# A decoder block's attention and forget gate rebuilt on one Trainium2 core: unsplit float32 q and k, scores on 64 rows, half-height transposes, values in one group, larger lumps

## The chip, the core and the metric

The kernel runs on one core of one Trainium2 chip. The metric is the device time of one execution in microseconds (us), the median of three runs. A profile of one execution comes with it: for each engine, when each instruction started, how long it took and what it waited for. The engines are PE (TensorE: matmuls, and PEld, its weight loads), DVE (VectorE), ACT (ScalarE), POOL (GpSimd) and SP, which issues the DMAs. Each engine works through its own queue in order.

## What is computed

One decoder layer on 256 tokens of width 1024 in float32, with two attention branches of 8 heads of 64 each:

```python
h = rms_norm(x, attn_norm_g)
qa, ka, va, qb, kb, vb, f_logit, g_logit = split(h @ w_in)
qa = rope(rms_norm(heads(qa), gq)); ka = rope(rms_norm(heads(ka), gk))   # branch 0
o_a = softmax(qa ka^T / 8, causal) va      # one block of 256 keys: plain causal attention
qb = rms_norm(heads(qb), gq2); kb = rms_norm(heads(kb), gk2)             # branch 1
c = cumsum(log_sigmoid(f_logit + b_forget))
o_b = softmax(qb kb^T / 8 + c[t] - c[s], causal) vb
x = x + (gate0 * (o_a @ w_moba) + gate1 * (o_b @ w_fox)) @ w_out
h2 = rms_norm(x, ffn_norm_g); u, g = split(h2 @ w_up)
x = x + (silu(conv3(g)) * u) @ w_down
```

## The kernel before

**Precision.** Weights and activations are split into a rounded float32r part and the rest (`whi` and `wlo`, `xh` and `xl`, `oh` and `ol`); a product is three float32r matmuls: hi by hi, hi by lo, lo by hi. ACT writes the hi part (L109 for weights), DVE the lo part (L110). Six buffers of each are in turn: a new one is split when PE has finished with the one six halves back. V, the probabilities and the transposes are plain float32. A plain float32 matmul of the code stands as two records in the trace, a transpose as one.

**Order.** PE's queue stands exactly as the code is written. The other engines' queues are laid out by a scheduler from data dependences. Weights come in chunks of 1 MB through three `raw` buffers.

**Stages on PE.** `project(m, pt, h)` does half of a 512-column projection (two weight halves, 24 matmul pairs, L212); m = 0, 1, 2 are q, k, v of branch 0, and 3, 4, 5 of branch 1. `norm1` (L190) sums the squares of x; DVE and ACT make `rs`, the row scale, of it (L177 to L182). `rs_row` (L408) spreads `rs` over a row. `forget_a` to `forget_d` and `forget_bias` make the decay bias of branch 1: `forget_a` multiplies x with the 8 forget columns (L283, L284: 16 matmuls with 16 columns of hi and lo weights), `forget_b` turns that (L293) and takes log-sigmoid, `forget_c` makes the cumulative sum (L322 to L324), `forget_d` sends it through DRAM to all partitions. `finish_qk` normalises q or k on DVE and ACT into `qn` (and for branch 0 applies rope, L237 to L240). `turn_qk` transposes it (8 transposes, L257) and writes the pieces qA, qB, kA for the split scores. `scores(br, pair)` (L362, L363) makes two heads' scores, each product in two float32r matmuls over 128 rows (hi and lo of k stacked on the rows), and then the softmax on DVE and ACT (L368 to L376); of 256 by 256 the upper right block is left out, so a head has 128 x 128 and 128 x 256. `turn(br, pair)` (L385) transposes the probabilities, six blocks of 128 x 128 a pair. `values(br, pair)` (L396) multiplies them with V, two heads side by side on 64 columns each. Then `gate(c)`, eight times, 48 float32r matmuls of 256 columns (L420 to L422).

These pieces are written between the projections and gates one pair at a time (L440 to L504), so that DVE and ACT have a projection's or a gate's time for each.

## Time and profile before

| | us |
|---|---|
| median of three runs | 386.28 |
| runs | 385.81 to 386.96 |
| span of the profiled execution (first to last instruction) | 377.5 |
| PE busy in the span | 369.2 |
| DVE, ACT, POOL busy in the span | 286.4, 227.9, 15.7 |
| branch attention and gates (45.97 to 148.62), length | 102.65 |

The profiled execution has no time of its own beside its span; the span is 8.8 us shorter than the median of the runs. A line of the timeline reads: start, length, engine, line of the code, operation, written tile <- read tiles, shape, count; several equal instructions in a row are one line, from the first start to the last end. The time in brackets is how long the engine sat idle ahead of it, and who ended that. Records of matmuls overlap, since PE takes up the next before the last has drained; so costs on PE are read from start to start.

### The profile page before, as it was taken

To read this page: it belongs to the slowest core of one execution; us is meant where nothing else is said; L and a number is where in the kernel's file an instruction comes from. 1 tells how busy PE (TensorE), PEld (TensorE's weight loads), DVE (VectorE), ACT (ScalarE), POOL (GpSimd) and SP (SyncE) were. 2 spreads that over 40 slices of the span, in tenths; PEclk is the share of its full clock that TensorE was granted. 3 is DMA by queue.
4 is the path that set the end of the run, shared out by engine and by line. 5 is a ranking of instruction groups with operands and counts; after the bars stand their busy time and mean duration, and the time that the engine had idled before them with its cause. 6 is when DMAs were issued, how large, how long until landed. Compare 5 with 4: busy or idle time off the path is not lost.

```text
span 377.5 us, 7103 instructions
## 1 busy us (share of the span) xinstructions
PE 369.2 (98%) x2893; PEld 346.9 (92%) x2893; DVE 286.4 (76%) x504; ACT 227.9 (60%) x382; POOL 15.7 (4%) x19
## 2 busy tenths in 40 slices
PE   7999999999999999999999999999999999999995
PEld 2778887879999999999999999999999999999995
DVE  3879989899987755787796968676776867778653
ACT  4938497678956795454578756454554545455520
POOL 2410000000000000000060000000000000000000
PEclk9999999999999999999999999999999999999999
DMA  6994740755363533544645545554465456545003
GB/s 200 359 368 160 258 163 7 264 184 190 138 222 126 212 114 111 208 159 192 225 153 182 214 167 184 221 214 168 178 222 198 159 202 224 194 157 207 3 0 111
DMA packets 12000, 68.11 MB, mean 180 GB/s; under 512 B 1592, under 2 KB 2240, under 8 KB 4416
## 3 DMA queue, kind: packets, MB, share of 16 engines
q1 hardware_dynamic: 11664, 66.60, 49.3%
q10 hardware_dynamic: 304, 1.06, 0.8%
q8 instruction: 22, 0.36, 0.4%
q14 instruction: 10, 0.08, 0.1%
HBM read 66.60 MB, written 1.06 MB: 179 GB/s over the span
## 4 chain that ended last, share of the span: by engine, by line
PE 86%; DVE 4%; DMA 3%; ACT 3%; SPq 1%; issue 1%; POOLq 0%; POOL 0%; ACTq 0%; DVEq 0%
PE bank L420 14%; PE bank L421 14%; PE bank L422 14%; PE bank L212 12%; PE bank L605 5%; PE bank L606 5%; PE bank L604 5%; DMA raw<-in_qkv 3%; PE bank L517 2%; PE bank L519 2%; PE bank L518 2%; DVE wlo L110 2%; PE bank L396 2%; PE bank L385 2%; PE bank L544 1%; PE bank L543 1%
## 5 line engine op out<-in xcount | busy, mean ns | idle before, releaser
L110 DVE TENSOR_TENSOR wlo<-raw,whi 128x1024 fp32r<-128x1024 f32 (+1 forms) x126 | 152.2, 1213 | 50.4 <-ACT whi L109 50.2
L109 ACT ACTIVATE whi<-raw 128x1024 fp32r<-128x1024 f32 (+1 forms) x126 | 129.1, 1029 | 84.1 <-PE bank L421 45.3
L421 PE MATMUL bank<-ol,whi 128*128 128x256 f32 x352 | 97.3, 276 | 0.1
L420 PE MATMUL bank<-oh,whi 128*128 128x256 f32 x352 | 97.4, 277 | 0.0
L422 PE MATMUL bank<-oh,wlo 128*128 128x256 f32 x352 | 97.2, 276 | 0.0
L421 PEld LDWEIGHTS bank<-ol,whi 128*128 128x128 f32 x352 | 66.1, 188 | 0.3 <-DVE ol L552 0.3
L420 PEld LDWEIGHTS bank<-oh,whi 128*128 128x128 f32 x352 | 66.1, 188 | 0.0
L422 PEld LDWEIGHTS bank<-oh,wlo 128*128 128x128 f32 x352 | 66.1, 188 | 0.0
L420 PE MATMUL bank<-xh,whi 128*128 128x256 f32 x128 | 36.2, 283 | 0.0
L422 PE MATMUL bank<-xh,wlo 128*128 128x256 f32 x128 | 35.9, 280 | 0.0
L421 PE MATMUL bank<-xl,whi 128*128 128x256 f32 x128 | 35.9, 280 | 0.0
L212 PE MATMUL bank<-whi,xh 128*128 128x512 f32 x96 | 30.6, 400 | 1.2 <-ACT whi L109 1.0
L212 PE MATMUL bank<-wlo,xh 128*128 128x512 f32 x96 | 30.3, 397 | 1.0 <-DVE wlo L110 1.0
L212 PE MATMUL bank<-whi,xl 128*128 128x512 f32 x96 | 29.8, 391 | 0.0
L422 PEld LDWEIGHTS bank<-xh,wlo 128*128 128x128 f32 x128 | 24.4, 190 | 0.0
L420 PEld LDWEIGHTS bank<-xh,whi 128*128 128x128 f32 x128 | 24.2, 189 | 0.2 <-issue 0.2
L421 PEld LDWEIGHTS bank<-xl,whi 128*128 128x128 f32 x128 | 24.0, 188 | 0.0
L212 PEld LDWEIGHTS bank<-wlo,xh 128*128 128x128 f32 x96 | 17.6, 188 | 6.6 <-DVE wlo L110 2.9
L212 PEld LDWEIGHTS bank<-whi,xh 128*128 128x128 f32 x96 | 17.2, 188 | 5.6 <-ACT whi L109 2.5
L212 PEld LDWEIGHTS bank<-whi,xl 128*128 128x128 f32 x96 | 18.0, 188 | 4.0
L573 DVE TENSOR_TENSOR sq<-bank,rs 128x512 f32<-128x512 f32 x22 | 15.1, 690 | 6.5 <-PE bank L422 6.5
L371 ACT ACTIVATE s<-s,nm 128x128 f32<-128x128 f32 (+1 forms) x32 | 14.2, 448 | 9.1 <-DVE nm L368 8.3
(171 smaller groups left out, 756.2 us busy)
## 6 DMA issues: line engine op xcount, KB each, us to landing
raw<-in_wu SPq DMA_DIRECT2D x22, 1024.0 KB, 4.8
raw<-in_wd SPq DMA_DIRECT2D x11, 1024.0 KB, 4.9
raw<-in_qkv SPq DMA_DIRECT2D x9, 1024.0 KB, 4.9
raw<-in_wg SPq DMA_DIRECT2D x8, 1024.0 KB, 5.3
raw<-in_wb SPq DMA_DIRECT2D x4, 1024.0 KB, 4.8
raw<-in_wo SPq DMA_DIRECT2D x4, 1024.0 KB, 4.7
raw<-in_qkv SPq DMA_DIRECT2D x8, 256.0 KB, 6.2
raw<-in_qkv SPq DMA_DIRECT2D x2, 512.0 KB, 6.6
```

The source lines that it names most:

```text
L109: nc.scalar.activation(hi[:, s], raw[:, s], AF.Copy)
L110: nc.vector.tensor_tensor(lo[:, s], raw[:, s], hi[:, s].bitcast(F32), op=ALU.subtract)
L212: nc.tensor.matmul(pt[t], lhs[:, k, t * P:(t + 1) * P], rhs, start=(k == 0 and i == 0), stop=(k == KT - 1 and i == 2))
L371: last_exp[:] = [nc.scalar.activation(s[:, j, c], s[:, j, c], AF.Exp, scale=-1.0, bias=nm[:, j, i:i + 1], accum_out=l[:, j, i:i + 1])]
L385: nc.tensor.transpose(tp[:, b * P:(b + 1) * P], s[:, j, b * P:(b + 1) * P], ident)
L420: nc.tensor.matmul(o, wh[:, w], mh[:, k], start=(k == 0 and i == 0), stop=False)
L421: nc.tensor.matmul(o, wh[:, w], ml[:, k], start=False, stop=False)
L422: nc.tensor.matmul(o, wl[:, w], mh[:, k], start=False, stop=(k == KT - 1 and i == 1))
L573: nc.vector.tensor_tensor(ev, up_.rearrange("p (b t) -> p b t", b=2), rs2[:, None, :].to_broadcast([P, 2, S]), op=ALU.mult)
L604: nc.tensor.matmul(o, wh[:, w], ah, start=(p == 0 and h == 0 and c == 0), stop=False)
L605: nc.tensor.matmul(o, wh[:, w], al, start=False, stop=False)
L606: nc.tensor.matmul(o, wl[:, w], ah, start=False, stop=(last and h == 1 and d == ds[-1]))
```

## The change

- q and k are no longer split: `turn_qk` writes plain float32 tiles qT and kT, one copy on ACT and one on DVE for a whole q or k (before: 24 and 16 pieces over the four calls; now 4 and 4).
- `scores` takes two pairs at a time. A head's product is one plain float32 matmul over its own 64 rows (two records in the trace); the two heads of a pair lie on the upper and the lower 64 rows, and write different banks.
- Transposes (`turn_qk`, `turn`) take 64 rows at a time: twice as many, each with 64 columns streamed instead of 128; upper and lower halves follow each other and write different banks.
- `values(br)` does all four pairs of a branch, two pairs to a bank; one copy and one subtraction then cover two pairs.
- `forget_a` uses unsplit x and weights: eight plain float32 matmuls of 32 columns, four column strips at once, placed with `rs_row` directly behind `norm1`. `forget_b` adds the four strips up with a selection matrix (`sel`, eight more columns of the constants) in two plain float32 matmuls.
- The order of the pieces is written anew; `s` and `pT` have four buffers instead of three and two. The FFN takes qT, kT and a third tile aT where it took qA, qB, kA.

```diff
-    for tag in ("qA", "qB", "kA"):
-        T([P, 2, 4, S], tag, 1, F32R)
+    for tag in ("qT", "kT", "aT"):
+        T([P, 4, S], tag, 1, F32R)
...
     def turn_qk(qn, br, isk):
         g = col(C_QG + 2 * br + isk)
-        for t in range(NT):
-            tp = bank()
+        tp = banks()
+        for t in range(NT):
             for b in range(4):
-                nc.tensor.transpose(tp[:, b * P:(b + 1) * P], qn[:, t, 2 * b:2 * b + 2].rearrange("p h d -> p (h d)"), ident)
...
-                nc.scalar.activation(hi, src, AF.Copy, scale=g[own])
...
-                nc.vector.scalar_tensor_tensor(lo, src, g[own], hi.bitcast(F32), op0=ALU.mult, op1=ALU.subtract)
+                for h, r in enumerate(halves):
+                    src = qn[r, t, 2 * b:2 * b + 2].rearrange("p h d -> p (h d)")
+                    nc.tensor.transpose(tp[h][:, (4 * t + b) * HD:(4 * t + b + 1) * HD], src, ident[r, r])
+        dst = (kT if isk else qT).rearrange("p b (t h c) -> p h t b c", t=NT, h=2)
+        for h in range(2):
+            src = tp[h].rearrange("p (t b c) -> p t b c", t=NT, b=4)
+            if h == 0:
+                nc.scalar.activation(dst[:, h], src, AF.Copy, scale=g)
+            else:
+                nc.vector.tensor_scalar_mul(dst[:, h], src, g)
...
+        wfg = T([P, KT, 32], "wfg")
+        nc.gpsimd.memset(wfg, 0.0)
+        nc.vector.tensor_tensor(wfg[:, :, 0:NH], wfr, g1[:, :, None].to_broadcast([P, KT, NH]), op=ALU.mult)
         fp = bank()
         for k in range(KT):
-            nc.tensor.matmul(fp[:16, :S], wf2[:, k], xh[:, k], start=(k == 0), stop=False)
-            nc.tensor.matmul(fp[:16, :S], wf2[:, k], xl[:, k], start=False, stop=(k == KT - 1))
+            r = slice(32 * (k % 4), 32 * (k % 4 + 1))
+            nc.tensor.matmul(fp[r, :S], wfg[:, k], xT[:, k], start=(k < 4), stop=(k >= 4))
...
-            nc.tensor.transpose(ft[:, t * 16:(t + 1) * 16], fs[:, t * P:(t + 1) * P], ident[:16, :16])
+            nc.tensor.matmul(ft[:, t * NH:(t + 1) * NH], fs[:, t * P:(t + 1) * P], sel, start=True, stop=True)
...
-                nc.tensor.matmul(dst, qA[:, j, pair, ts], kA[:, j, pair, us], start=True, stop=False)
-                nc.tensor.matmul(dst, qB[:, j, pair, ts], kA[:, j, pair, us], start=False, stop=True)
+    def scores(br, pairs):
+        sps = [banks() for _ in pairs]
+        for t in range(NT):
+            ts, us = slice(t * P, (t + 1) * P), slice(0, (t + 1) * P)
+            for pair, sp in zip(pairs, sps):
+                for j, r in enumerate(halves):
+                    nc.tensor.matmul(sp[j][:, t * P:t * P + (t + 1) * P], qT[r, pair, ts], kT[r, pair, us], start=True, stop=True)
+        for pair, sp in zip(pairs, sps):
+            softmax(br, pair, sp)
...
-                nc.tensor.transpose(tp[:, b * P:(b + 1) * P], s[:, j, b * P:(b + 1) * P], ident)
+                for h, r in enumerate(halves):
+                    nc.tensor.transpose(tp[h][:, (3 * j + b) * HD:(3 * j + b + 1) * HD], s[r, j, b * P:(b + 1) * P], ident[r, r])
...
+    def values(br):
+        for pp in range(2):
+            op = bank()
+            for i, c in enumerate((slice(0, 256), slice(256, 384))):
+                for q in range(2):
+                    pair = 2 * pp + q
+                    for j, r in enumerate(halves):
+                        vc = br * W4 + (2 * pair + j) * HD
+                        nc.tensor.matmul(op[r, q * S + i * P:(q + 1) * S], V[:, i, vc:vc + HD], probs[br, pair][:, j, c],
+                                         start=(i == 0 and q == 0), stop=(i == 1 and q == 1))
```

The new order of the calls, from `norm1` to the last gate:

```python
norm1(); rs_row(); forget_a(); qn = finish_qk(pq, 0, 0); project(1, pk, 1)
kn = finish_qk(pk, 0, 1); project(2, pv, 0); forget_b(); turn_qk(qn, 0, 0)
project(2, pv, 1); turn_qk(kn, 0, 1); finish_v(pv, 0); project(3, pq, 0)
forget_c(); scores(0, (0, 1)); project(3, pq, 1); qn = finish_qk(pq, 1, 0)
forget_d(); scores(0, (2, 3)); project(4, pk, 0); turn(0, 0); turn(0, 1)
project(4, pk, 1); kn = finish_qk(pk, 1, 1); turn(0, 2); turn(0, 3); turn_qk(qn, 1, 0)
project(5, pv, 0); forget_bias(); values(0); project(5, pv, 1); turn_qk(kn, 1, 1)
finish_v(pv, 1); gate(0); scores(1, (0, 1)); gate(1); scores(1, (2, 3)); gate(2); gate(3)
turn(1, 0); turn(1, 1); gate(4); turn(1, 2); turn(1, 3); gate(5); values(1); gate(6); gate(7)
```

Three places show what moved. First PE's queue at `norm1`, before the change (the row with L190; L212 is `project(1, pk, ...)`):

```order
L212 MATMUL bank_204<-whi_171,xl_84 128x512
L212 MATMUL bank_205<-whi_171,xl_84 128x512
L190 MATMUL bank_296<-ones1_153,bias_159 128x1 x2
L212 MATMUL bank_204<-whi_177,xh_83 128x512
L212 MATMUL bank_205<-whi_177,xh_83 128x512
L212 MATMUL bank_204<-wlo_178,xh_83 128x512
```

and now (L191 is `norm1`, L409 `rs_row`, L279 `forget_a`, L213 the projection):

```order
L213 MATMUL bank_201<-whi_171,xl_84 128x512
L213 MATMUL bank_202<-whi_171,xl_84 128x512
L191 MATMUL bank_293<-ones1_153,bias_159 128x1 x2
L409 MATMUL bank_311<-cst_185,rs_189 128x128 x2
L279 MATMUL bank_318<-xT_82,wfg_315 32x256 x8
L213 MATMUL bank_201<-whi_177,xh_83 128x512
```

`rs_row` and `forget_a` have moved ahead of the half projection that stood behind `norm1`.

Second, PE's queue at the first `turn_qk`, before: it stands (L257) at the end of `project(2, pv, 1)`, and `project(3, pq, 0)` follows.

```order
L212 MATMUL bank_207<-whi_340,xl_84 128x512
L257 MATMUL bank_519<-cst_185,qn_314 128x128 x4
L257 MATMUL bank_530<-cst_185,qn_314 128x128 x4
L212 MATMUL bank_543<-whi_358,xh_83 128x512
L212 MATMUL bank_544<-whi_358,xh_83 128x512
```

Now it stands at the end of `project(2, pv, 0)`, behind `forget_b` (L288); the first two of its 16 rows, one for each half:

```order
L213 MATMUL bank_203<-whi_259,xl_84 128x512
L213 MATMUL bank_204<-whi_259,xl_84 128x512
L288 MATMUL bank_449<-cst_185,pT_327 128x8 x2
L257 MATMUL bank_471<-cst_185,qn_329 128x64
L257 MATMUL bank_472<-cst_185,qn_329 128x64
```

It has moved a half projection forward, and with it k's `turn_qk`, which now ends `project(2, pv, 1)`.

Third, DVE's queue ahead of the first `qn`, before, from its multiplication with the norm (L230) to rope's last row (L240); L110 are weight splits, L177 and L180 belong to k:

```order
L230 TENSOR_TENSOR qn_314<-bank_202,qf_322 128x512
L230 TENSOR_TENSOR qn_314<-bank_203,qf_322 128x512
L177 TENSOR_SCALAR qfv_409<-ss_401 128x16
L110 TENSOR_TENSOR wlo_427<-raw_356,whi_426 128x1024
L237 TENSOR_TENSOR p1_334<-qn_314,rc0_306 128x256
L238 TENSOR_TENSOR p2_335<-qn_314,rsn0_307 128x256
L180 SCALAR_TENSOR_TENSOR qfv_409<-qfv_409 128x16
L110 TENSOR_TENSOR wlo_445<-raw_442,whi_444 128x1024
L239 TENSOR_TENSOR qn_314<-p1_334,p2_335 128x16x8
L240 TENSOR_TENSOR qn_314<-p1_334,p2_335 128x16x8
```

and now (L231 to L241; L226 belongs to k):

```order
L231 TENSOR_TENSOR qn_329<-bank_199,qf_337 128x512
L231 TENSOR_TENSOR qn_329<-bank_200,qf_337 128x512
L110 TENSOR_TENSOR wlo_374<-raw_371,whi_373 128x1024
L238 TENSOR_TENSOR p1_349<-qn_329,rc0_303 128x256
L239 TENSOR_TENSOR p2_350<-qn_329,rsn0_304 128x256
L226 TENSOR_REDUCE ss_390<-sq_394 128x8
L240 TENSOR_TENSOR qn_329<-p1_349,p2_350 128x16x8
L241 TENSOR_TENSOR qn_329<-p1_349,p2_350 128x16x8
```

One weight split fewer stands between, and one fewer ahead of these rows: five in place of seven from `rs` on.

More of the change, by code (lines that the diff above doesn't have):

```diff
@@ L162, in decoder_block @@
     load(7)
-    cst = T([P, 832], "cst")
+    cst = T([P, 840], "cst")
     nc.sync.dma_start(cst, a["consts"])
@@ L169, in decoder_block, with rsqrt_mean @@
     cos2 = cst[:, 768:832].rearrange("p (t c) -> p t c", t=NT)
+    sel = cst[:, 832:840]
     wfr = T([P, KT, NH], "wfr")
     nc.sync.dma_start(wfr, a["wf"])
-    def rsqrt_mean(dst, ss, n, shape, tag):
-        w = T([P, 3] + shape, tag, 2)
+    def rsqrt_mean(dst, ss, n, shape, tag, bufs=2):
+        w = T([P, 3] + shape, tag, bufs)
         v, y, t = w[:, 0], w[:, 1], w[:, 2]
@@ L351, in decoder_block, with softmax @@
     last_exp = []
-    def scores(br, pair):
-        s = T([P, 2, 384], "s", 3)
+    def scores(br, pairs):
[7 more added lines that the diff above has]
+            softmax(br, pair, sp)
+    def softmax(br, pair, sps):
+        s = T([P, 2, 384], "s", 4)
         nm = T([P, 2, 2], "nm", 4)
         l = T([P, 2, 2], "l", 4)
-        sps = banks()
-        for t in range(NT):
-            for j in range(2):
-                dst = sps[j][:, t * P:t * P + (t + 1) * P]
-                ts, us = slice(t * P, (t + 1) * P), slice(0, (t + 1) * P)
-                nc.tensor.matmul(dst, qA[:, j, pair, ts], kA[:, j, pair, us], start=True, stop=False)
-                nc.tensor.matmul(dst, qB[:, j, pair, ts], kA[:, j, pair, us], start=False, stop=True)
         for j in range(2):
@@ L444, in decoder_block @@
     norm1()
+    rs_row()
+    forget_a()
     qn = finish_qk(pq, 0, 0)
     project(1, pk, 1)
-    rs_row()
-    forget_a()
     kn = finish_qk(pk, 0, 1)
@@ L451, in decoder_block @@
     forget_b()
+    turn_qk(qn, 0, 0)
     project(2, pv, 1)
-    turn_qk(qn, 0, 0)
+    turn_qk(kn, 0, 1)
     finish_v(pv, 0)
@@ L456, in decoder_block @@
     project(3, pq, 0)
-    turn_qk(kn, 0, 1)
+    forget_c()
+    scores(0, (0, 1))
     project(3, pq, 1)
-    forget_c()
-    scores(0, 0)
     qn = finish_qk(pq, 1, 0)
+    forget_d()
+    scores(0, (2, 3))
     project(4, pk, 0)
-    forget_d()
-    scores(0, 1)
+    turn(0, 0)
+    turn(0, 1)
     project(4, pk, 1)
-    turn(0, 0)
-    scores(0, 2)
     kn = finish_qk(pk, 1, 1)
+    turn(0, 2)
+    turn(0, 3)
+    turn_qk(qn, 1, 0)
     project(5, pv, 0)
-    values(0, 0)
-    turn(0, 1)
+    forget_bias()
+    values(0)
     project(5, pv, 1)
-    scores(0, 3)
-    turn_qk(qn, 1, 0)
+    turn_qk(kn, 1, 1)
     finish_v(pv, 1)
-    values(0, 1)
-    turn(0, 2)
-    forget_bias()
     gate(0)
-    turn(0, 3)
-    turn_qk(kn, 1, 1)
-    values(0, 2)
+    scores(1, (0, 1))
     gate(1)
-    values(0, 3)
-    scores(1, 0)
+    scores(1, (2, 3))
     gate(2)
-    scores(1, 1)
     gate(3)
     turn(1, 0)
-    scores(1, 2)
+    turn(1, 1)
     gate(4)
-    values(1, 0)
-    turn(1, 1)
-    scores(1, 3)
+    turn(1, 2)
+    turn(1, 3)
     gate(5)
-    values(1, 1)
-    turn(1, 2)
+    values(1)
     gate(6)
-    values(1, 2)
-    turn(1, 3)
     gate(7)
@@ L503, in decoder_block @@
         gate_sigmoid(c)
-    values(1, 3)
     mh = T([P, KT, S], "xh", 1, F32R)
```

64 lines of the change are left out of this document (21 added, 43 removed).

## The prediction

> **What bounds the kernel now.** I read the page's busy times and its chain that ended last first, then the stretch from the first branch's attention to its end, then the timeline of TensorE (PE) in that stretch.
>
> ```profile
> span 377.5 us, 7103 instructions
> PE 369.2 (98%) x2893; PEld 346.9 (92%) x2893; DVE 286.4 (76%) x504; ACT 227.9 (60%) x382; POOL 15.7 (4%) x19
> PE 86%; DVE 4%; DMA 3%; ACT 3%; SPq 1%; issue 1%; POOLq 0%; POOL 0%; ACTq 0%; DVEq 0%
> 45.97:148.62 102.65, 102.29 (x740) 92.11 (x738) 85.42 (x203) 80.01 (x169) 0.00 (x0) 1.00 0.46 164
> ```
>
> The last row gives, for the stretch from 45.97 to 148.62 with nearly all attention in it, the busy time of PE, PEld (weight loads), DVE, ACT and POOL, then PE's granted clock. PE is busy 98% of the span and 102.29 of 102.65 us there; the clock is 1.00. So I count PE's time from one start to the next, and work of DVE and ACT only where PE waits for it. The many ACT and DVE instructions that the change drops count for nothing by themselves. Behind 148.62 (branch projections, output, FFN) PE issues the same instructions in the same order; I carry that stretch over whole.
>
> **The change, part by part.** First what the new PE order waits for.
>
> ```profile
> 25.47 0.51 PE L190 MATMUL bank<-ones,bias 128*128 128x1 f32 x4
> 25.83 0.70 PE L212 MATMUL bank<-whi,xh 128*128 128x512 f32 x2
> 27.07 0.16 DVE L182 SCALAR_TENSOR_TENSOR rs<-rsv 128x2 f32<-128x2 f32 x1
> 31.41 0.61 PE L408 MATMUL bank<-cst,rs 128*128 128x128 f32 x4
> 31.78 0.36 PE L283 MATMUL bank<-xh,wf 128*16 128x256 f32 x1
> 33.73 0.63 PE L212 MATMUL bank<-whi,xh 128*128 128x512 f32 x2
> 39.34 0.29 PE L293 MATMUL bank<-cst,pT 16*128 16x16 f32 x2
> 39.56 0.74 PE L212 MATMUL bank<-whi,xh 128*128 128x512 f32 x2
> ```
>
> *rs.* norm1's matmuls are followed at 25.83 by a projection; rs is written at 27.07 + 0.16 = 27.23. The change puts rs_row, which reads rs, directly behind norm1, and the projection behind that. PE waits from 25.83 to about 27.28: **+1.45**. Behind the waiting matmul stand forget_a, the projection and all the rest of PE's queue; DVE and ACT are free for this chain in both, and their own queues go on.
>
> *forget_a.* Today 31.78 to 33.73 = 1.95. The rate of a plain f32 matmul is L408's: four records (two per matmul written) spaced (0.61 - 0.27)/3 = 0.11 for 128 columns. New: eight matmuls of 256 columns = 4 x 0.11 = 0.44 each, four of them side by side on column strips, so two rounds, 0.88, and 0.1 to change over: **-0.95**. If only two strips ran at once it would be -0.1.
>
> *forget_b.* Today 0.22 (39.34 to 39.56). Two plain f32 matmuls with 128-column loads are four records; below, L323's two records take 0.22, so 0.44 and the gap ahead: **+0.15**. PE thus reaches turn_qk(qn) at 39.56 + 1.45 - 0.95 + 0.15 = 40.2; today it comes there a half projection later.
>
> ```profile
> 31.27:48.16 16.89, 16.89 (x90) 13.76 (x89) 16.78 (x41) 11.74 (x18) 0.00 (x0) 1.00 0.67 243
> 28.99 2.36 DVE L110 TENSOR_TENSOR wlo<-raw,whi 128x1024 fp32r<-128x1024 f32 x2 [0.26 <-ACT whi L109]
> 41.14 1.22 DVE L110 TENSOR_TENSOR wlo<-raw,whi 128x1024 fp32r<-128x1024 f32 x1
> 42.47 0.29 DVE L240 TENSOR_TENSOR qn<-p,p 128x128 f32<-128x128 f32 x1
> 45.17 1.04 PE L257 MATMUL bank<-cst,qn 128*128 128x128 f32 x8
> 45.97 0.71 PE L212 MATMUL bank<-whi,xh 128*128 128x512 f32 x2
> 47.87 0.29 DVE L240 TENSOR_TENSOR qn<-p,p 128x128 f32<-128x128 f32 x1
> ```
>
> *q's wait.* qn is ready at 42.47 + 0.29 = 42.76 today, and DVE has no gap from 31 us on (16.78 busy of 16.89 in the first row, behind PE and PEld). Between rs and this L240 stand seven splits L110 (the first two and the last are shown), in the new order five; one takes 2.36 - 1.22 = 1.14 of DVE's time, so qn comes 2.3 earlier, at about 40.5: wait **+0.3**.
>
> *k's wait.* PE then does turn_qk(qn) (0.66 by the price below) and a half projection (5.5, 33.73 to 39.34 less the gap), so it is at turn_qk(kn) at 40.5 + 0.66 + 5.5 = 46.7. Today kn is ready at 47.87 + 0.29 = 48.16, and PE asks for it only behind another half projection. DVE's list ahead of kn is nearly as long in the new order (qT's evacuation is added, two small forget steps go). PE waits about 1.5 and starts there at 48.2. Queued behind it on PE is everything else. Today's PE had qn turned and started the next projection at 45.97; so up to here **+2.2**, in which all terms above are contained. Bounds: no wait for q and k, +0.4; kn two us later, +4.2.
>
> *A wait that goes.* Scores(0, 0) waits for kA today: **-0.4**. kT's two evacuations now stand a projection ahead of their use.
>
> ```profile
> 59.31 0.30 PE L362 MATMUL bank<-kA,qA 128*128 128x128 f32 x1 [0.36 <-DVE kA L269]
> 58.09 0.37 PE L323 MATMUL bank<-lf,cst 128*128 128x8 f32 x2
> 58.31 0.37 PE L324 MATMUL bank<-lf,cst 128*128 128x8 f32 x2
> 103.67 0.28 PE L422 MATMUL bank<-xh,wlo 128*128 128x256 f32 x1
> 103.89 0.87 PE L396 MATMUL bank<-pT,V 128*64 128x256 f32 x8
> 104.69 0.33 PE L362 MATMUL bank<-kA,qA 128*128 128x128 f32 x1
> 105.71 0.28 PE L420 MATMUL bank<-xh,whi 128*128 128x256 f32 x1
> 111.36 0.22 PE L362 MATMUL bank<-kA,qA 128*128 128x128 f32 x1
> 112.29 0.28 PE L420 MATMUL bank<-xh,whi 128*128 128x256 f32 x1
> ```
>
> *values.* One call writes eight records: four of 256 and four of 128 columns, 12 x 0.11 = 1.32 if each followed the last; PE is through in 0.80 (103.89 to 104.69). So the two 64-column strips do run side by side (0.66), and 0.1 goes at either end. With the gap ahead (103.79 to 103.89) a call costs 0.9, eight 7.2. New, per branch: 24 x 0.11 = 2.64 per strip and 0.2 for the ends, twice: 5.7. **-1.5**, the change-overs.
>
> *scores.* A head pair costs 1.02 (104.69 to 105.71) and 0.93 (111.36 to 112.29); eight some 7.6. New: each head has 64 rows to itself; 128 + 256 columns in two records each, 6 x 0.11 = 0.66, both heads at once; a lump of two pairs 1.32 and 0.15 to change over, four lumps 5.9: **-1.7**. The trace shows strips side by side in columns only, not in rows. Bounds: no overlap, 11.2 (+3.6); overlap of streams but not of loads (0.11 each by L323, two by two 0.22, four times a head pair), 7.6 (no gain). I take the overlap because it is nearest to L396.
>
> *Transposes.* Eight whole ones take 0.80 (45.17 to 45.97), 0.11 each; 72 remain behind turn_qk(kn)'s start, 7.8. Each becomes two of 64 rows and 64 columns.
>
> ```profile
> 39.34 0.20 PEld L293 LDWEIGHTS bank<-cst,pT 16*128 16x128 f32 x2 [0.36 <-DVE qfv L177]
> L385 PEld LDWEIGHTS bank<-cst,s 128*128 128x128 f32 x48 | 5.3, 140 | 1.0 <-DVE gates L427 0.3 <-issue 0.2 <-DVE nm L368 0.2
> L293 PE MATMUL bank<-cst,pT x2: 207/218/230, 39.3 to 39.4; 16*128 16x16 f32 x2
> ```
>
> Call T the time of two halves. The stream is half as long: 0.055 if both run at once, the lower bound. The load stays 128 columns: L293's two loads (16 rows) start 0.20 - 0.14 = 0.06 apart, and a whole one in L385 is as long (140 ns), so a load costs 0.06 however few rows: T = 0.12 if the halves load in turn. L293's two matmuls start 0.29 - 0.207 = 0.08 apart (the later is the shorter): T = 0.16 if each half costs that. I take T = 0.07, nearest to the overlap seen in L396, with a little for twice the instructions. 72 x 0.07 = 5.0, and seven lumps at 0.15: 6.1, **-1.7**.
>
> The Trainium skill, "TensorE: Matmul & The Clock Gate", section "LDWEIGHTS (loading the stationary operand)", speaks against this part: a load's time goes by its columns, 128 / 1.2 = 107 ns, and 32 rows take as long as 128. On the rows the trace agrees (L293 beside L385); on the figure it agrees for plain f32 (L323, 0.11) and not for transposes (0.06). By its figure T would be 0.107 at best and this part +1.0 where I have -1.7, so the sum -0.4.
>
> Everything that leaves ACT and DVE (20 of 24 q and k copies on ACT, 12 of 16 on DVE, half of the oh and ol splits) lies beside PE's work, and costs PE nothing there. pT and s get four buffers, so the four pairs of a branch wait for no older one. forget_d's two DMAs stay on ACT's queue, half a projection earlier, and its buffer, one of the three raw ones, is held until forget_bias as before; eight more columns of the constants are nothing in a load of 832.
>
> Sum: 2.2 - 0.4 - 1.5 - 1.7 - 1.7 = **-3.1**. The profiled span of 377.5 becomes 374.4. The median of the three runs is 386.28, 8.8 above the span, start and end that the trace does not hold; with the same 8.8 I get **383.2**.
>
> **The rivals.**
>
> *Slower: the halves do not overlap.* Place: scores and every transpose. Point: with the other terms as they are, T over 0.113 makes the kernel slower. If only loads follow one another, T = 0.12 (9.7, +1.9) and scores gain nothing: 2.2 - 0.4 - 1.5 + 0 + 1.9 = +2.2, **388.5**. If the streams do too, scores are +3.6: +5.8, **392.1**. Against it: L396's overlap. For it: no two records of the trace share the array by rows. The Trainium skill, same page, "Part 3: Packing small matmuls — row/col tiling", says that loads overlap running matmuls when the row group differs; no run here shows that yet, and it takes chance from this rival.
>
> *Each half costs an issue of 0.08.* T = 0.16, 12.6, +4.8 on the transposes: +3.4, **389.7**. For it: L293's spacing. Against: L396's eight records and eight loads pass in 0.80, 0.05 for each of the sixteen, and their streams set that.
>
> *The load sets the spacing.* T = 0.11, as a whole transpose: 9.0, +1.2, sum -0.2, **386.1**, no change.
>
> *The waits grow.* DVE is busy 85.42 of 102.65 us from 45.97, and two pairs' softmax must now be done before a lump of turns. If kn comes two us later, or turn(0, 2) waits as long for DVE, -3.1 becomes -0.5 to -1: **385.6**.
>
> **How the numbers follow.** Forecast 0.54; the halves do not overlap 0.14; issue 0.08; load spacing 0.11; waits 0.13. Within the forecast the time goes from 380.3 (T = 0.055, another -1.1, and no wait for q and k, -1.8) to 385. 0.3% is 1.16 us, about what a measurement of this kernel can tell from no change. Faster by more: nearly all of the forecast and a part of waits, 0.59. Within: load spacing, most of waits, 0.19. Slower: 0.22. The range reaches from 380.2 to 388.5; it leaves out the streams in turn, issue, and a tail below.
>
> **What would show it.** L409 (rs_row) with 1.4 us of PE idle ahead; L257 waiting for DVE's qn, some 0.3 and 1.5; 16 records of L257 in about 0.6 and 24 of L381 in 0.85 (0.07 a pair) against 0.88 and 1.3 (0.11); eight score matmuls (16 records) in 1.3 against 2.6; L395's 32 records in 2.7. The prediction fails if halves start only after one another, if PE stands before turn(0, 2), or if something behind 148.62 moves by more than the sum.

## The result, and the profile after

| us | before | after |
|---|---|---|
| executions compared first | 386.28, 385.81, 386.96, 387.15 | 385.49, 384.85, 376.54, 377.91 |
| median | 386.62 | 381.38 |
| span of the profiled execution | 377.5 | 383.7 |

The four executions of before against the two lower ones of after gave a ratio of 0.976 (0.973 to 0.979): 9.2 us faster, where 3.1 were forecast. The new times fall into two groups 8 us apart, and a number of this case can be understood only with that: executions of either kernel come in a lower and an upper group, and what lies between the groups is not the change.

The first sign stands in the page of the kernel after. Its profiled execution is 6 us longer than the one of before, though the kernel is faster.

```profile
span 383.7 us, 7223 instructions
PE 373.3 (97%) x2975; PEld 348.9 (91%) x2975; DVE 277.8 (72%) x486; ACT 214.4 (56%) x357; POOL 14.2 (4%) x18
PE 80%; DVE 9%; DMA 5%; ACT 3%; issue 1%; SPq 1%; POOLq 0%; POOL 0%; ACTq 0%; DVEq 0%
```

PE is still what bounds it. The table of stretches shows where the 6 us are. Columns: stretch, its length, busy time and (number of records) of PE, PEld, DVE, ACT, POOL, then PE's granted clock, DMA share, GB/s. First three stretches of before, then the same of after: norm1 to the first k turn, from there to the branch outputs, from there to the FFN's second block.

```profile
25.47:45.97 20.50, 20.50 (x108) 16.81 (x106) 18.70 (x46) 13.16 (x21) 0.00 (x0) 1.00 0.62 225
45.97:148.55 102.58, 102.22 (x739) 92.05 (x737) 85.42 (x203) 79.94 (x169) 0.00 (x0) 1.00 0.46 164
148.55:198.71 50.16, 49.59 (x434) 49.19 (x433) 39.23 (x55) 27.95 (x42) 7.61 (x7) 1.00 0.51 181
```

```profile
26.03:48.60 22.57, 20.17 (x117) 15.92 (x115) 20.84 (x55) 14.90 (x26) 0.00 (x0) 1.00 0.53 200
48.60:146.64 98.04, 97.67 (x809) 85.92 (x809) 73.90 (x177) 64.35 (x141) 0.00 (x0) 1.00 0.47 168
146.64:198.16 51.52, 51.06 (x434) 50.86 (x432) 39.75 (x55) 28.69 (x41) 7.71 (x7) 1.00 0.52 186
```

The first two stretches are where the change is: +2.07 and -4.54, so -2.5. The third has the same 434 matmuls in both kernels and takes 1.4 longer. One stretch of the FFN, of before and of after:

```profile
300.00:350.00 50.00, 50.00 (x444) 50.00 (x442) 36.52 (x50) 26.78 (x38) 0.00 (x0) 1.00 0.54 190
```

```profile
300.00:350.00 50.00, 50.00 (x427) 50.00 (x426) 34.90 (x49) 25.75 (x36) 0.00 (x0) 1.00 0.52 183
```

PE is busy for all 50 us in both, at clock 1.00, with the same instructions, and 444 matmuls fall into them in the one and 427 in the other: 0.113 us from start to start against 0.118. Over the 1535 matmuls from 199 us to the end that is 6.8 us (199.36 to 373.23 against 198.82 to 379.49). Nothing is waited for. I call these the two paces; a block of 48 matmuls takes 5.44 at the one and 5.65 at the other.

The places that the prediction named, in the timeline of PE after:

```profile
26.03 0.51 PE L191 MATMUL bank<-ones,bias 128*128 128x1 f32 x4
27.85 0.71 PE L409 MATMUL bank<-cst,rs 128*128 128x128 f32 x4 [1.31 <-DVE rs L183]
28.49 1.07 PE L279 MATMUL bank<-xT,wfg 128*32 128x256 f32 x16
29.49 0.73 PE L213 MATMUL bank<-whi,xh 128*128 128x512 f32 x2
...
40.59 0.51 PE L288 MATMUL bank<-cst,pT 128*128 128x8 f32 x4
41.16 0.71 PE L257 MATMUL bank<-cst,qn 64*128 64x64 f32 x16
41.80 0.73 PE L213 MATMUL bank<-whi,xh 128*128 128x512 f32 x2
...
48.60 0.71 PE L257 MATMUL bank<-cst,qn 64*128 64x64 f32 x16 [1.02 <-DVE qn L241]
...
62.97 1.58 PE L351 MATMUL bank<-kT,qT 64*128 64x128 f32 x16
64.48 0.72 PE L213 MATMUL bank<-whi,xh 128*128 128x512 f32 x2
...
70.18 0.96 PE L381 MATMUL bank<-cst,s 64*128 64x64 f32 x24
71.07 0.73 PE L213 MATMUL bank<-whi,xh 128*128 128x512 f32 x2
...
84.47 2.82 PE L395 MATMUL bank<-pT,V 128*64 128x256 f32 x32
87.22 0.74 PE L213 MATMUL bank<-whi,xh 128*128 128x512 f32 x2
```

They stand nearly as named, but q's wait of 0.3 is missing (0.07): 1.3 us of idle ahead of rs_row, 1.0 ahead of the k turn, 16 half transposes in 0.64, 24 in 0.89, a lump of scores in 1.51, a branch's values in 2.75.

### The profile page after: what moved, and what is told of

Read it like the earlier page. It is cut to its first block, busy times and chain, and to the rows that moved or that the text cites. A ratio compares the mean times of both kernels' runs of the same rounds, so it can differ in the third digit from the quotient of the medians.

```text
span 383.7 us, 7223 instructions
## 1 busy us (share of the span) xinstructions
PE 373.3 (97%) x2975; PEld 348.9 (91%) x2975; DVE 277.8 (72%) x486; ACT 214.4 (56%) x357; POOL 14.2 (4%) x18
## 4 chain that ended last, share of the span: by engine, by line
PE 80%; DVE 9%; DMA 5%; ACT 3%; issue 1%; SPq 1%; POOLq 0%; POOL 0%; ACTq 0%; DVEq 0%
PE bank L421 14%; PE bank L423 14%; PE bank L422 14%; PE bank L213 7%; PE bank L597 5%; PE bank L595 5%; PE bank L596 5%; DMA raw<-in_qkv 3%; DVE wlo L110 3%; PE bank L508 2%; PE bank L509 2%; PE bank L510 2%; DMA raw<-in_wg 1%; PE bank L395 1%; PE bank L534 1%; PE bank L535 1%
## 5 line engine op out<-in xcount | busy, mean ns | idle before, releaser
L110 DVE TENSOR_TENSOR wlo<-raw,whi 128x1024 fp32r<-128x1024 f32 (+1 forms) x126 | 152.3, 1213 | 63.1 <-ACT whi L109 61.9
L421 PE MATMUL bank<-oh,whi 128*128 128x256 f32 x352 | 99.1, 281 | 0.0
L422 PE MATMUL bank<-ol,whi 128*128 128x256 f32 x352 | 99.0, 281 | 0.0
L423 PE MATMUL bank<-oh,wlo 128*128 128x256 f32 x352 | 98.9, 281 | 0.0
L422 PEld LDWEIGHTS bank<-ol,whi 128*128 128x128 f32 x352 | 67.5, 192 | 0.0
L423 PEld LDWEIGHTS bank<-oh,wlo 128*128 128x128 f32 x352 | 66.1, 188 | 0.0
L421 PEld LDWEIGHTS bank<-oh,whi 128*128 128x128 f32 x352 | 66.1, 188 | 0.0
L421 PE MATMUL bank<-xh,whi 128*128 128x256 f32 x128 | 36.3, 284 | 0.0
L422 PE MATMUL bank<-xl,whi 128*128 128x256 f32 x128 | 35.7, 279 | 0.0
L423 PE MATMUL bank<-xh,wlo 128*128 128x256 f32 x128 | 35.7, 279 | 0.0
L213 PE MATMUL bank<-whi,xh 128*128 128x512 f32 x96 | 31.6, 410 | 1.2 <-ACT whi L109 0.8
L213 PE MATMUL bank<-wlo,xh 128*128 128x512 f32 x96 | 30.6, 400 | 1.2 <-DVE wlo L110 1.1
L213 PE MATMUL bank<-whi,xl 128*128 128x512 f32 x96 | 29.8, 392 | 0.0
L421 PEld LDWEIGHTS bank<-xh,whi 128*128 128x128 f32 x128 | 24.1, 188 | 1.0 <-issue 0.5
L213 PEld LDWEIGHTS bank<-whi,xh 128*128 128x128 f32 x96 | 17.5, 190 | 7.5 <-ACT whi L109 2.2
L423 PEld LDWEIGHTS bank<-xh,wlo 128*128 128x128 f32 x128 | 24.2, 189 | 0.0
L213 PEld LDWEIGHTS bank<-wlo,xh 128*128 128x128 f32 x96 | 17.9, 190 | 6.9 <-DVE wlo L110 3.4
L422 PEld LDWEIGHTS bank<-xl,whi 128*128 128x128 f32 x128 | 24.0, 188 | 0.0
L213 PEld LDWEIGHTS bank<-whi,xl 128*128 128x128 f32 x96 | 18.1, 188 | 4.1
L508 PE MATMUL bank<-oh,whi 128*128 128x256 f32 x64 | 18.0, 281 | 0.0
```

The lines of the kernel that those rows point to most:

```text
L110: nc.vector.tensor_tensor(lo[:, s], raw[:, s], hi[:, s].bitcast(F32), op=ALU.subtract)
L213: nc.tensor.matmul(pt[t], lhs[:, k, t * P:(t + 1) * P], rhs, start=(k == 0 and i == 0), stop=(k == KT - 1 and i == 2))
L421: nc.tensor.matmul(o, wh[:, w], mh[:, k], start=(k == 0 and i == 0), stop=False)
L422: nc.tensor.matmul(o, wh[:, w], ml[:, k], start=False, stop=False)
L423: nc.tensor.matmul(o, wl[:, w], mh[:, k], start=False, stop=(k == KT - 1 and i == 1))
L508: nc.tensor.matmul(o, wh[:, w], oh[:, 4 * br + k], start=(k == 0), stop=False)
```

## Experiments: the two paces

### Both kernels again, unchanged

> The kernel before, unchanged. In its profiled execution the 1535 matmuls of the FFN (199.36 to 373.23) start 0.1133 us apart; in that of the kernel after they start 0.1178 us apart (198.82 to 379.49), with the same instructions. Theory A (two paces): an unbroken run of 256-column float32r matmuls goes at one of two paces, 0.1133 or 0.1178, whichever it falls into at the break ahead of it, and either kernel can fall into either. Then some executions of this kernel have a span near 377.5 and a time near 379.3 (1.8 around the span, as in the kernel after), the others 385.8 to 387.2, some 8 us apart, and none lies in between. Theory B (the change makes the pace): this kernel in its timed runs always goes at 0.1178; all times 385.8 to 387.2 and the profile of before was an exception. Theory C (8.8 us lie around the span of this kernel): spans near 377.5 at times near 386.

> The kernel after, unchanged. Theory A: two groups of times, near 377 and near 385; at the same pace it is faster than the kernel before by 1.5 to 3 us (the branch outputs began at 146.64 against 148.55). Theory B: mostly near 377. Stage by stage both theories want the same up to the first gate: it begins near 93.6.

Measured on one chip: before 380.12, 386.07, 378.80, 378.82, 379.17, 379.37, and as the partner in the same rounds 7 times 378.65 to 379.79 and 4 times 385.76 to 386.64. After: 385.08, 384.80, 376.57, 377.34, 376.87, 377.66. Every time is its span and 1.7 to 1.9 us (386.07: 384.3; 378.80: 377.0). Theories B and C fall: the kernel before has both groups, and 1.8 us lie around the span, not 8.8. Over all runs of this study 46 of 100 executions of before lay at 385.4 to 387.5 and 54 at 378.4 to 380.9, none between; of after, 4 of 10 lay in the upper group. (Two executions of before, 412.7 and 528.9, and one other, 2076.9, stand apart from everything and are left out.) In the first comparison all four of before lay in the upper group, while its profile had been one of the lower. Within the lower group the change is worth 0.9947 (0.9932 to 0.9962): **-2.0 us**, from 1.4 to 2.6.

### Is the pace a matter of the whole execution?

The 32 blocks of the FFN, each with one small matmul ahead of it, whose result nobody uses:

```diff
+        if kind == "A":
+            nc.tensor.transpose(d[:, 0:P], ident, ident)
+        if kind == "B":
+            nc.tensor.matmul(d[:, 0:P], ident, ident, start=True, stop=True)
+        if kind == "C":
+            nc.tensor.matmul(d[:, 0:P], hh[:, 0, 0:P], hh[:, 1, 0:P], start=True, stop=True)
...
+        if kind == "E":
+            nc.tensor.matmul(d[:, 0:HD], hh[:, 0, 0:P], hh[:, 1, 0:HD], start=True, stop=True)
```

> The kernel after, with one small matmul of unused result ahead of each run of 48 matmuls in the FFN (32 places): in turn a transpose of 128 x 128 (A), a plain float32 matmul of 128 columns (B), a float32r matmul of 128 columns (C), or nothing (D is one of 256 columns, as the stream's own). Theory A (two paces, fallen into at a break): the pace changes between 0.1133 and 0.1178 only behind some of these places, and stays behind a D; 48 matmuls take 5.44 or 5.65 us. If each kind sets a pace of its own, the same kind is always followed by the same pace. If it shifts a phase, the pace behind a kind depends on the pace ahead. Rival: the pace belongs to a whole execution (the chip is slower for its length), then all 32 runs of 48 have one pace whatever stands between.

> The same with two other kinds: one float32r matmul of 64 columns (E), or two of 128 columns (F). Expected as for the run before it: by theory A the pace changes behind some, by the rival behind none.

Timeline of the second run, around its first four inserted matmuls (L572 is E, L575 is F):

```profile
197.61 0.37 PE L421 MATMUL bank<-oh,whi 128*128 128x256 f32 x1
...
203.35 0.34 PE L575 MATMUL bank<-oh 128*128 128x128 f32 x2
203.52 0.33 PE L421 MATMUL bank<-oh,whi 128*128 128x256 f32 x1
...
209.23 0.20 PE L572 MATMUL bank<-oh 128*128 128x64 f32 x1
209.26 0.36 PE L421 MATMUL bank<-oh,whi 128*128 128x256 f32 x1
...
214.81 0.19 PE L572 MATMUL bank<-oh 128*128 128x64 f32 x1
```

From a block's first matmul to the next inserted one: 203.35 - 197.61 = 5.74, then 5.71, then 5.55. (A break lengthens the block behind it by up to 0.1, so here 5.51 to 5.55 is the fast pace, 0.1133 in the middle of the block, and 5.65 to 5.74 the slow one, 0.1178.) The pace changed at 209.23, in the middle of one execution, and all blocks from there on took 5.51 to 5.55 (the last, with the program's end, 5.68). So the pace doesn't belong to the execution; it belongs to an unbroken run of matmuls, and a break can change it. In the other run it changed 19 times: blocks took 5.54 behind each of eight B, 5.65 to 5.66 behind D, behind C 5.70 where the block ahead was fast and 5.52 where it was slow, behind A 5.74 six times and 5.54 twice. D, which looks like one more matmul of the stream, turned fast into slow (B, 5.540, D, 5.653). Neither "a kind sets its pace" nor "a kind shifts a phase" covers all of that, but behind the third block E and F never led out of the fast pace, in 29 breaks.

### Is it drawn at the wait ahead of the FFN?

Ahead of the FFN PE waits 0.4 to 0.5 us for POOL's squares. This edit takes the wait out, and leaves the FFN's norm out of the result:

```diff
-            nc.tensor.matmul(sp[:, 0:S], ones, sqs, start=True, stop=True)
+            nc.tensor.matmul(sp[:, 0:S], ones, cst[:, 0:S], start=True, stop=True)
```

> The kernel before; the matmul that sums the squares for the FFN's norm reads a constant tile in place of sqs (so the FFN's norm is left out of the result), and no longer waits 0.35 to 0.5 us for POOL. The 1535 matmuls behind it are the long run whose pace differs between executions. If the pace is drawn at this wait, whose end comes at any moment of PE's clock, then without the wait PE's whole course from 52 us on is the same in every execution and the times form one group (spread under 1.5 us), near 379 or near 386. If the pace is drawn elsewhere (ahead of it, or during the run), two groups 7 us apart remain.

> The same edit in the kernel after. Its last wait ahead of the FFN is then the one for kn at 48 us or for the weights. If the pace is drawn at the wait for POOL: one group. If it is drawn at any wait, two groups may remain, and the runs of 48 in the gates (5.65 or 5.85 us) show it: their sequence was the same in four traces of this order and the other way round in four.

Before without the wait: 378.48, 378.45, and 384.90 to 386.40 four times; two groups remain. After without it: 382.44 to 385.42, spans 380.7 to 383.6, and the one traced has the FFN at 5.65. None lay in the lower group. So the theory that the pace is drawn at this wait falls for the kernel before; for the kernel after, with one group in six executions, it stays open. The gates show an earlier part of it: in before they take the same times to 0.01 us in all five traces (5.746, 5.851, 5.656, ...), while after has two courses. In one the first two gates take 5.646 and 5.851 and the branch outputs 45.23; in the other 5.848, 5.640 and 43.52. The eight traces with the same order up to there show the first course three times and the second five times. In before the branch outputs always take 43.64 (43.86 with a B ahead of them, below).

### Can it be led? First try: B

One plain float32 matmul ahead of the branch outputs (`if c == 0`) and one ahead of the FFN's second block (`if f == 1`), written where the block's own matmuls write next.

> The kernel before with one plain float32 matmul of 128 columns (unused result; kind B of the run before) ahead of the branch outputs and one ahead of the FFN's second block. Behind B the pace was 0.1133 in 8 of 8 places. Theory A: it sets the pace, so that no execution is slow: all near 379.5 (the fast ones of before, and 0.24 for each B), none near 386. If B went with the fast pace only by its neighbours in that run, executions near 386 remain.

> The kernel after with the same two matmuls at the same two places. Theory A: no execution near 385; and since all parts that the change doesn't touch now go at one pace in both kernels, the difference between this and the run before it is the change by itself. The profiles put it at -2.0 (both branch outputs begin: 146.3 to 146.6 against 148.6 to 149.4, so -2.0 to -3.1) up to there; the prediction had -3.1. So 376.5 to 377.5 against 379.5. Rival (the change is worth 9 us by itself, as the first comparison showed): 370 against 379.5.

Before: ten executions at 379.31 to 380.65, four at 386.65 to 387.76. Its trace is from the upper group:

```profile
149.62:193.48 43.86, 43.86 (x388) 43.86 (x387) 33.86 (x49) 23.88 (x36) 2.99 (x3) 1.00 0.51 179
219.00:355.00 136.00, 136.00 (x1157) 136.00 (x1156) 95.61 (x129) 69.38 (x98) 0.00 (x0) 1.00 0.52 187
```

1157 in 136 us are 0.1175 apart: the slow pace, right behind a B. That B sets the pace was a guess from eight places with like neighbours, and it falls. After with B: five at 376.47 to 378.01, too few to tell. Lower group against lower group it is 0.9943 (0.9923 to 0.9964) of the unchanged kernel before.

### Second try: E, four times

```diff
+        if 1 <= f <= 4:
+            nc.tensor.matmul(sp[:, S:S + HD], hh[:, 0, 0:P], hh[:, 1, 0:HD], start=True, stop=True)
```

> The kernel before with one float32r matmul of 64 columns (kind E, unused result) ahead of each of the FFN's blocks 1 to 4. In the run with E and F, 28 of 28 runs of 48 behind the first three stayed at the fast pace once it was reached, and of three matmuls at the slow pace one (an E) brought it. If E leads into the fast pace and keeps it, executions of this kernel have 0.5 us more than the fast ones of before (379.5 to 380.5), and the slow group near 386 is gone or rare. If that run only happened to fall so, a third to a half of the executions remain near 386.5.

> The kernel after with the same four matmuls. If E leads into the fast pace: nearly all executions at 376.8 to 378.5, none near 385, and against the run before it the change by itself, 2 to 3 us. If not, a group near 385 remains.

Before: nine executions, 380.44 to 381.76. After: twelve, 377.61 to 380.53. None in the upper group in 21, where 46 of 100 and 4 of 10 had been. Medians 380.94 and 378.94: again -2.0. The first E cost 1.0 us more than its own time, since it writes into the bank of the sum of squares while DVE reads it.

### A version faster than both on average

E written into the columns that its block overwrites next, so that it waits for nobody, ahead of gate(6), of the branch outputs and of FFN blocks 1 to 3:

```diff
+    def lead(dst, m):
+        nc.tensor.matmul(dst[:, 0:HD], m[:, 0, 0:P], m[:, 1, 0:HD], start=True, stop=True)
...
+        if c == 6:
+            lead(gp, xh)
...
+        if c == 0:
+            lead(bp[0], oh)
...
+        if 1 <= f <= 3:
+            lead(up_, hh)
```

> The kernel after with E (one float32r matmul of 64 columns, unused result) ahead of gate(6), of the branch outputs and of the FFN's blocks 1 to 3, written into the columns that the block's own matmuls overwrite next. In the two runs before, the first E stood 1.0 us behind the sum of squares (1.349 in place of 0.348), since DVE was still reading that bank; here it waits for nobody. If that and 0.14 for each E is all that it costs: 5 x 0.14 = 0.7 on the fast executions of the kernel after (374.7 to 376.2 of span), up to 2.1 off those whose branch outputs go at the slow pace; so 376 to 378 in every execution, one group, faster than both kernels on average. If E does not lead ahead of the branch outputs, the spread stays as in the run before, 377 to 379.5; if the wait of 1.0 was what made the fast pace sure, a group near 385 comes back.

Seven executions, 376.63 to 378.19, median 377.37; 0.9936 (0.991 to 0.9962) of the lower group of before. The ten of after average 380.3, these seven 377.4. The trace shows the leading at work (L426 is E):

```profile
196.10 0.36 PE L421 MATMUL bank<-oh,whi 128*128 128x256 f32 x1
...
201.84 0.20 PE L426 MATMUL bank<-oh 128*128 128x64 f32 x1
201.87 0.36 PE L421 MATMUL bank<-oh,whi 128*128 128x256 f32 x1
...
207.41 0.19 PE L426 MATMUL bank<-oh 128*128 128x64 f32 x1
207.44 0.37 PE L421 MATMUL bank<-oh,whi 128*128 128x256 f32 x1
```

Behind the first E the block was slow (5.74), behind the second fast (5.54), and all the FFN stayed so. In the four traces with E in the FFN the first E left its block slow twice, a later one never. What the E ahead of gate(6) and of the branch outputs does is not shown: the traced execution was on the faster course before them. Against the lower group of after (mean 377.1) this version gains nothing; its gain is that none of the seven lay in the upper group, where before lay 9 times of 12 in the same rounds.

## Experiments: the attention stage

### Half-height transposes

The kernel after with transposes of 128 rows:

> The kernel after with transposes of 128 rows again (8 a call of turn_qk, 6 a turn), everything else as it is. If halves side by side are what made the transposes cheap (16 records of turn_qk in 0.64 us, 24 of two turns in 0.89), turn_qk takes 0.79 again (+0.15, four times), two turns 1.26 to 1.30 (+0.4, four times): +2.2 in all, the first gate 1.0 to 1.4 later. If the halves gain nothing and the larger lumps do, two turns stay near 0.9 and nothing moves.

Timeline: two turns and the q turn of branch 1.

```profile
70.87 1.47 PE L379 MATMUL bank<-cst,s 128*128 128x128 f32 x12
77.69 1.47 PE L379 MATMUL bank<-cst,s 128*128 128x128 f32 x12
79.00 1.04 PE L256 MATMUL bank<-cst,qn 128*128 128x128 f32 x8
```

Two turns took 1.31 from start to start (79.00 - 77.69; the other 1.23), against 0.79 and 0.89 with halves; turn_qk 0.79 to 0.85 against 0.64. Over four and four that is 2.2, as expected. In the trace of after (k's turn) the two halves' records start 4 ns apart and the next pair 60 ns later. So T is 0.06, and the halves do overlap. The Trainium skill's figure ("TensorE: Matmul & The Clock Gate", section "LDWEIGHTS (loading the stationary operand)"), 107 ns for 128 columns, would not allow that: for transposes the trace does not agree.

### Scores on 64 rows

> The kernel after, with the score matmuls of a lump written head by head, so that two in a row use the same 64 rows twice before the other rows are used. If halves overlap only because they stand side by side in the queue, half of the pairs no longer overlap and a lump takes 1.9 to 2.5 us in place of 1.51, four lumps 1.6 to 4 more. If the 64 rows alone make a score cheap, a lump stays at 1.51.

> The kernel after with all eight records of the upper 64 rows of a lump ahead of all eight of the lower. Written two by two a lump took 1.61 against 1.51, and the records still started in pairs. If the halves overlap over four records but not over eight, a lump takes 2.5 (8 x 0.105 + 8 x 0.211, the steps of a pair by its columns) in place of 1.51, four lumps 4 more: that is what side by side is worth. If 64 rows are cheap by themselves, it stays near 1.6.

```diff
-            for pair, sp in zip(pairs, sps):
-                for j, r in enumerate(halves):
+            for j, r in enumerate(halves):
+                for pair, sp in zip(pairs, sps):
```

The second run has that loop over j outside the loop over t. Lumps took 1.61 and 2.06 in place of 1.51. Neither took as long as no overlap would (1.9 to 2.5, and 2.5). In the run with eight of a half first, the lower half's first record (known by its 128 columns, where the upper half is at its last four, of 256) starts at 62.320, behind the upper half's fifth (62.315) and ahead of its sixth (62.533): by these starts PE looks about four records ahead, and starts a matmul for free rows past those that wait for theirs. The overlap is real, and the order in the code matters less than expected. What a lump takes with no overlap was not seen.

### Are the new waits a cost of the order?

Four kernels put the starts of rs_row, forget_a and the turns elsewhere. First rs_row and forget_a back where before has them, and turn_qk(kn) half a projection later:

> The kernel after with rs_row and forget_a put back behind the next half projection, and turn_qk(kn) half a projection later (ahead of forget_c). By the prediction's terms the wait for rs (1.31 us in the profile after) goes, and the wait for kn (1.02) goes; the first scores come right behind and may wait 0.3 to 0.5 for kT. So the first gate begins at 91.4 to 92.2 in place of 93.58. If these waits only move on (DVE is what is late, and the softmax of two pairs becomes late in its turn), it begins at 93 or later and a wait stands ahead of turn(0, 0). The total moves by the same 1.5 to 2 us at equal pace, and by 8 us more between paces.

One execution at 379.60, five at 386.77 to 387.88: later than after in both groups. PE's timeline at its longest wait and behind it:

```profile
42.95 1.11 PE L257 MATMUL bank<-cst,qn 64*128 64x64 f32 x16 [3.86 <-DVE qfv L182]
43.99 1.22 PE L213 MATMUL bank<-whi,xh 128*128 128x512 f32 x2
45.01 1.05 PE L213 MATMUL bank<-wlo,xh 128*128 128x512 f32 x2
```

The rs wait was gone, and the q turn waited 3.9 instead: qn was written at 42.8 on DVE's list, in after at 41.0. PE without the pause asks for weight splits sooner, and between rs and qn DVE's list now has seven of them, 1.2 each, where in after it has five. Then all starts as in before, and the same with every later piece of the attention half a projection later (and with two B in it):

> The kernel after with rs_row, forget_a, turn_qk(qn) and turn_qk(kn) all put back to where the kernel before had them; scores follow forget_c. The 3.9 us wait for qn that came up when only two of them were moved should go, since qn then has another half projection of time. If the waits for rs and kn (1.31 and 1.02 us) are what the new order costs, and the larger lumps cost nothing, the first gate begins at 91.3 to 92.3 in place of 93.2 to 93.6, and the time at equal pace falls by 1 to 2 us against the kernel after. If DVE's list is what decides, a new wait of 1 us or more stands ahead of the first scores or of the first turns, and nothing is gained.

> The kernel after with the starts of rs_row, forget_a and the first turn_qk as in the kernel before, and every later piece of attention half a projection later (scores of the first two pairs behind project(3, pq, 1), their turns behind project(4, pk, 1), and so on), with one B ahead of gate(6) and one ahead of the FFN's second block. If the waits for rs and kn (1.31 and 1.02 us) then have no successor, gates begin 1.5 to 2.3 earlier than in the kernel after; B ahead of gate(6) takes 0.4 off two gates. So 374.5 to 375.5 in every execution. If waits only move, as in the run with scores right behind forget_c, a wait of 1 us or more stands ahead of the first scores or turns: 376 to 377.

The first has its lower group at 375.99 to 377.39, 0.9919 (0.9892 to 0.9946) of before; its first gate begins 67.6 us behind norm1, in the traces of after's order 67.3 to 68.1. By the trace nothing is gained, and the interval overlaps that of after: forget_c now took 2.08 in place of 0.66, and the scores waited 1.2. The second is slower than before, 1.0077 (1.0041 to 1.0114): the q turn of branch 1 waited 2.7 for the copies of the turns ahead.

```profile
PE bank L351 <- DVE cc L317: 1.2, 1, 1.2
```

```profile
80.40 0.59 PE L381 MATMUL bank<-cst,s 64*128 64x64 f32 x12
81.50 0.97 PE L381 MATMUL bank<-cst,s 64*128 64x64 f32 x12 [0.52 <-DVE s L371]
85.16 1.59 PE L257 MATMUL bank<-cst,qn 64*128 64x64 f32 x16 [2.69 <-ACT pT L384]
```

Last, both starts a quarter projection later:

> The kernel after with rs_row and forget_a in the middle of project(1, pk, 1) and turn_qk(kn) in the middle of project(3, pq, 0), a quarter projection (2.8 us) later each; all else in its order. If the two waits (1.31 and 1.02 us) are the order's own cost, the first gate begins 1.5 to 2.3 earlier after norm1 than in the kernel after (67.4 to 67.6). If DVE is what limits this stretch, they come back as other waits, as in the two runs before with later starts: less than 0.5 earlier.

1.0054 (1.0029 to 1.0078) of before: a wait of 4.4 for qn. All four attempts to save the 2.3 us of waits brought them back elsewhere. In three traces the longest wait was for DVE, in the one with everything later for ACT's copies. The first gate came 67.6 us behind norm1 in one and 71.8 to 72.0 in the other three; none of the four is shown to be better than the order of the kernel after.

## Why the prediction was off

The forecast was 383.2; the executions of after were near 377 and near 385. The step that failed is the last: "The median of the three runs is 386.28, 8.8 above the span, start and end that the trace does not hold". Only 1.8 lie around the span. The other 7.0 were the FFN's slow pace, in which those three runs were and the profiled execution was not; the one trace of an upper execution of before, that with two B, has its FFN blocks at 5.65, and all ahead of the FFN as in the others. Span 374.4 and 1.8 would have been 376.2, against 376.5 to 377.9 measured in the lower group. The first comparison's 9.2 us then set four executions of one kernel's upper group against two of the other's lower group. That the median of after, 381.38, lies between the 380.3 and 385 that the forecast allowed for is luck: it is the middle of two groups, and no execution of after was near it.

The sum itself was -3.1, and the change by itself is -2.0. Term by term, start to start in the two profiles:

| term | forecast | measured |
|---|---|---|
| wait for rs | +1.45 | +1.45 (0.37 to 1.82, norm1 to rs_row) |
| rs_row itself | 0 | +0.27 (0.37 to 0.64) |
| forget_a | -0.95 | -0.96 (1.96 to 1.00) |
| forget_b | +0.15 | +0.35 (0.22 to 0.57) |
| waits for q and k | +0.3, +1.5 | +0.07, +1.02 |
| all to the k turn's start | +2.2 | +2.07 |
| wait for kA | -0.4 | -0.36 |
| values | -1.5 | -0.9 (8 calls, 6.41, to 2 of 2.75) |
| scores | -1.7 | -2.2 (8.20 to 4 lumps of 1.51) |
| transposes | -1.7 | -1.9 (7.67 to 5.79, a wait of 0.36 behind one of them included) |
| the six half projections behind the k turn, in their first and last matmuls | 0 | +0.87 (33.36 to 34.23) |
| forget_c, forget_d | 0 | +0.25 |
| gates | 0 | -0.35 (45.85 to 45.50; their pace) |
| to the branch outputs | -3.1 | -2.5 |
| behind, up to the FFN | 0 | -0.1 to +1.4, by the course |

- *Halves side by side* was right, with T = 0.06 for 0.07, and the three rivals built on T over 0.1 fall. Shown by the starts, and by undoing it.
- *Values* was mis-sized: the price of 0.9 a call held a gap ahead that belongs to the projection or gate, and that gap stayed. The half projections were put at nothing; the last four of the six now take 0.13 to 0.27 longer each. These two terms are 1.5 us short of the forecast. Scores gave 0.5 of it back, since the price before was mis-sized too (7.6, from two calls of 1.02 and 0.93, whose mean makes 7.8, where the eight take 8.20), transposes 0.2 (7.8 before, where 72 x 0.11 is 7.9 and the trace has 7.67), and the gates 0.35, by their pace: that the -2.5 is so near to the -3.1 is in part luck.
- *"Behind 148.62 ... I carry that stretch over whole"* was wrong. Same instructions, but the branch outputs take 43.5 or 45.2 in after, and always 43.6 in before. The slow course makes the stretch up to the FFN's second block 1.4 longer (51.52 for 50.16). With three of eight traces on it that is an estimated +0.5 on average, and -2.5 and +0.5 agree with the -2.0 measured. Both traces of the unchanged kernel after are of the upper group and on the slow course; -2.5 and +1.4 make -1.1 there, and upper against upper the kernels lay 1.2 apart (386.15 and 384.94 on average, only two executions of after).
- *Waits:* the forecast had their places and nearly their sizes. It charged them to the new order; in the four kernels with other orders they came back elsewhere, mostly where DVE was late.
- The prediction said it would fail if something behind 148.62 moved by more than the sum. That is what happened (the FFN alone differs by 6.8 between the two profiles), by a mechanism that no rival named.

What sets the pace at a break stays open. Shown is that it can change at any matmul put in between, that the clock, the waits and the DMA share don't go with it (1.00 and none at both; a share of 0.52 at the fast pace in the second trace of before and at the slow one in after), that the wait for POOL is not its only source, and that with three or four E at the head of the FFN none of 28 executions lay in the upper group.

## What to carry to other kernels

Before a span and a median are subtracted, ask whether they come from the same group: a difference of several per cent between a profile and its runs is a finding to explain, not a constant to carry. Where a long run of equal matmuls bounds a kernel, compare matmuls per microsecond between traces; two paces with the same instructions mean that a small change's gain can be hidden or multiplied, and a few short matmuls at the head of the run may settle it for 0.14 us each (a block of 5.58 in place of 5.44 here). And a wait that shows up with a new order need not be the order's to save: where the engine waited for is late anyway, moving the waiting piece moved the wait in all four orders tried here, and in three made it longer.

## What the hardware showed that was not expected

- Two paces of 256-column float32r matmuls, 0.1133 and 0.1178 us, at granted clock 1.00. A block repeats three kinds of matmul (hi by hi, lo by hi, hi by lo). At the slow pace the weight loads of one of the three are longer, 192 ns in place of 188 (the FFN's groups in the page of after; mean ns behind the comma):

```profile
L422 PEld LDWEIGHTS bank<-ol,whi 128*128 128x128 f32 x352 | 67.5, 192 | 0.0
L423 PEld LDWEIGHTS bank<-oh,wlo 128*128 128x128 f32 x352 | 66.1, 188 | 0.0
L421 PEld LDWEIGHTS bank<-oh,whi 128*128 128x128 f32 x352 | 66.1, 188 | 0.0
```

From 220 to 350 us every load of that kind reads 192 and every other one 187 or 188. Which kind it is differs between slow executions of one order: L422 here, L423 in the second trace of after, L421 in the one without the wait. At the fast pace all three read 187 or 188. So a run at the slow pace seems to keep a fixed place in the pattern of three; that this place is what sets the pace is not shown.

- A long wait of PE cost twice here. In the kernel with the 3.9 us wait the granted clock (third number from the end) fell to half and stayed there for 6 us of work; the two half projections behind took 13.66 in place of 11.1:

```profile
40.00:42.00 2.00, 0.00 (x0) 0.00 (x0) 2.00 (x5) 0.20 (x1) 0.00 (x0) 1.00 0.46 61
42.00:43.00 1.00, 0.05 (x2) 0.08 (x3) 1.00 (x6) 0.00 (x0) 0.00 (x0) 0.74 0.59 246
43.00:44.00 1.00, 1.00 (x17) 0.88 (x17) 1.00 (x6) 0.43 (x2) 0.00 (x0) 0.50 1.04 442
...
48.00:50.00 2.00, 2.00 (x8) 1.58 (x7) 0.25 (x2) 0.51 (x1) 0.00 (x0) 0.67 1.01 426
50.00:52.00 2.00, 2.00 (x10) 1.66 (x9) 1.22 (x1) 0.56 (x1) 0.00 (x0) 1.00 0.03 12
```

The Trainium skill, "TensorE: Matmul & The Clock Gate", section "What's actually happening", has PE's clock at half after at least one idle window of some 3.4 us, and back at full after at least one busy window as long. The falls behind waits of 3.9 and 4.4 agree; the way back took about 6 us here. And a wait of 2.7 was enough where PE had worked only 1.0 of the 4.2 us up to its end (all starts half a projection later, q turn at 85.16):

```profile
82.00:85.00 3.00, 0.47 (x8) 0.21 (x6) 3.00 (x6) 0.48 (x2) 0.00 (x0) 0.77 0.00 0
86.00:87.00 1.00, 1.00 (x16) 0.88 (x13) 1.00 (x3) 0.66 (x2) 0.00 (x0) 0.50 0.77 319
```

- PE ran matmuls past one another: in the kernel with eight records of a half first, a matmul on free rows started ahead of three that stood before it in the program and waited for the other rows.
